# Hybrid decoder trunk, first block: where the gate constants are loaded, and the meta tokens' state as a piece of its own

## The chip, the cores and the metric

The kernel runs on one core of a Trainium2 chip. The core has five engines with a queue of instructions each: TensorE (PE in the profile, with its weight loads listed apart as PEld), VectorE (DVE), ScalarE (ACT), GpSimd (POOL) and SyncE (SP, which here does nothing but start transfers), and 16 DMA engines that all queues share. The metric is the device time of one execution in microseconds (us). A kernel's time is the median of several runs. A profile is taken of one further execution, whose own time and span are given with it.

## The reference

One layer of a hybrid decoder. Sixteen meta tokens are put ahead of 2048 tokens of 1024 channels, the rows are normalised, and one input projection feeds two branches: a Mamba-2 state-space branch (SSD, 16 heads in 4 groups, state 128) and gated linear attention (GLA, 4 heads). Each branch starts from a state that the meta tokens alone make. The branches' outputs are normalised, projected, weighted by sigmoid gates, added, projected again and added to the input.

```python
u = rmsnorm(h, norm_w)
z, xbc, dt_raw, q, k, v, g_gla, a_lr, merge_g = split_cols(u @ w_in, IN_WIDTHS)
xbc = silu(causal_depthwise_conv(xbc, conv_w, conv_b))      # -> xs, bm, cm per head
y_m, s_m = ssd_chunked(xs[:, :m], dt[:, :m], a, bm[:, :m], cm[:, :m], N_META, s0)   # meta tokens
y_r, _   = ssd_chunked(xs[:, m:], dt[:, m:], a, bm[:, m:], cm[:, m:], SSD_CHUNK, s_m)
...
gate_logit = a_lr @ gla_gate_w2 + gla_gate_b                # low-rank gates of GLA
o_m, st_m = gla_chunked(q[:, :m], k[:, :m], v[:, :m], log_a[:, :m], N_META, st0)
o_r, _    = gla_chunked(q[:, m:], k[:, m:], v[:, m:], log_a[:, m:], GLA_CHUNK, st_m)
...
return hres + (sigmoid(merge_g) * branch_proj).sum(2) @ w_out
```

## The kernel before

**Two phases.** The first goes through the 2048 tokens in four blocks of 512 (the first block has the 16 meta tokens beside them: 528 columns) and makes the branch outputs, which go to HBM. The second multiplies by the gate, branch and output weights. The change lies in the first block of the first phase.

**Products in three parts.** A weight tile is loaded raw (tile `wr`, 3 buffers, line 173), its rounded high part is made on ACT (line 163), the remainder on POOL (line 164); both lie in a tile `whl` (4 buffers). A product is three matmuls, high by high, high by low, low by high (lines 183 to 185). In the first block every weight tile is also written back to HBM in its two parts (line 179) so that later blocks can fetch it ready (line 159). The write-back lags two tiles behind: at each new tile the third last is stored, and then the new raw tile is loaded. Both are started by SP.

**Units and pieces.** A block is eight units: four SSD groups (`ssd_proj`, i from 0 to 3) and four GLA heads (`gla_proj`). A unit is a generator that yields six times. An SSD unit yields halfway through its gate projection z, after z, and after each of its four feature tiles (two of x, one each of B and C; 48 matmuls of 264 columns in the first block, evicted by ACT into `cin` and `acc`, convolved by DVE at line 477, and finished by ACT line 480 and DVE line 481 as a tile `act`). After each yield `step()` lets every running background generator go on to its own next yield. In this document the stretch from one yield to the next is a piece.

**Background work.** `ssd_scan(g)` starts when group g's projection is done and so runs beside the unit that follows. Its pieces before the change: (1) fetch the decay rows; (2) transposes and the meta tokens' inputs (lines 503 to 511), the scores of the block (522), `before(0)`; (3) `meta_state()`, then `before(1)` and `after(0)`; (4) `before(2)`, `after(1)`; (5) `before(3)`, `after(2)`; (6) `after(3)`; (7) the row norm (589) and its scaling on ACT (591); (8) transposes (596) and the store. `before(c)` is transposes (538), scalings on DVE (541 to 544) and decays on ACT and DVE (550 to 553). `after(c)` multiplies (562), reads the state `s_ssd` on PE (563), forms the chunk's own contribution (565) and updates the state. `meta_state()` is one product on PE (515) and one copy on DVE (517) that writes `s_ssd`. It runs in the first block alone. `gates` starts at unit 1 and makes the GLA gates for the whole block: transposes (419), a product with the constant `w2` (432), Abs, Exp and Ln on ACT (435, 437, 438), a subtraction and cumulative sums on DVE (441, 443).

**Order.** PE and SP run in the order in which the program is written. For ACT, DVE and POOL a planner with its own cost model fixes the order when the kernel is built. Every engine then executes its list in order: an instruction whose input is late holds up all behind it. The same is true of SP: a load whose buffer isn't free yet holds up every later load.

**Buffers that matter.** `acc` has 2 buffers; each feature tile of the convolution takes one until line 481 has read it. `act` has 8 (`NACT`); in the first block they first hold the eight transposed pieces of the input (line 291), later the feature tiles and the gates' operand. `tok4` has 5 and `cb` has 3. `late_constants()` (lines 330 to 338) loads the low-rank gate weight three times into one staging tile, makes `w2` from it on ACT and DVE, loads the masks into a `tok4` tile and casts them to bytes on DVE. It is called once, ahead of unit 1.

Of the kernel before, what the change touches and what calls it, by code (L numbers as in the profile page):

```python
# [7 lines left out]
F32 = mybir.dt.float32  # L8
# [6 lines left out]
P = 128  # L15
D = 1024
KT = 8
META = 16
BLK = 512
NCH = BLK // P  # L20
SG = 4
# [6 lines left out]
NACT = 8  # L28
# [12 lines left out]
def trunk_kernel(ctx: ExitStack, tc: tile.TileContext, xm, xmt, w_feat, w_tok, w_zm, w_br, w_o,  # L41
# [7 lines left out]
    def mk(pool, shape, dt, tag, **kw):  # L49
        cnt[0] += 1  # L50
        return pool.tile(shape, dt, tag=tag, name=f"{tag}_{cnt[0]}", **kw)
# [52 lines left out]
    for s in range(nsb):  # L104
        b = 2 * s + 2
# [12 lines left out]
    wk = first.enter_context(tc.tile_pool(name="wk", bufs=2))  # L118
# [6 lines left out]
    def bank(pool, tag):  # L125
        return mk(pool, [P, 512], F32, tag)
# [49 lines left out]
    def save(n):  # L176

        while len(unsaved) > n:
            nc.sync.dma_start(*unsaved.pop(0))
# [19 lines left out]
    def proj_tok(key, src, u, starts, banks, width=256, per=2, sub=None):  # L199

        nq = KT // per
        opened = set()
        for q0 in range(0, nq, 2):
            if q0 == nq // 2:
                yield
            ws = [load_w(f"{key}_{q}", src[:, q * per * width:(q + 1) * per * width]) for q in (q0, q0 + 1)]
            for i, ((bk, ps), a) in enumerate(zip(banks, starts)):
                c0 = sub if sub is not None and i >= NCH else 0  # L210
                for k2 in range(2 * per):
                    kt = q0 * per + k2
                    h, lo = ws[k2 // per]
                    cs = slice(k2 % per * width + c0, (k2 % per + 1) * width)
                    accum(ps[:, c0:width], tuple(t[:, kt, a:a + P] for t in u),
                          (h[:, cs], lo[:, cs]), bk not in opened, kt == KT - 1, skip_group_check=True)
                    opened.add(bk)
# [86 lines left out]
    def fetch_u(b):  # L304
        next_u[b] = yield from load_u(b)
# [22 lines left out]
    msk = const.tile([P, NMSK, P], U8, name="msk")  # L328

    def late_constants():  # L330
        w2r = mk(wk, [P, META + BLK], F32, "acc")[:48, :512]
        for i in range(3):
            nc.sync.dma_start(w2r[16 * i:16 * i + 16, :], gw2)
        nc.scalar.activation(w2, w2r, AF.Copy)
        nc.vector.tensor_tensor(w2[32:48], w2r[32:48], w2[32:48].bitcast(F32), op=ALU.subtract)
        mstg = mk(wk, [P, D], F32, "tok4", bufs=NT4)[:, :NMSK * P]
        nc.sync.dma_start(mstg, cmsk)
        nc.vector.tensor_copy(msk.rearrange("p l t -> p (l t)"), mstg)
# [109 lines left out]
    def ssd_proj(o, g):  # L448
        m0, tt = o.m0, o.tt
        feats = []  # L450
        zs = mk(wk, [P, NCH, 256], F32, "tok4", bufs=NT4)
        if g == 0:
            pss = [bank(*pl) for pl in [(pj, "pj")] * 3 + [(pt, "pt")] + ([(pc, "pc")] if m0 else [])]
            yield from proj_tok("zm", w_zm, o.u, o.starts + [0] * o.ci0, list(enumerate(pss)), 288, 1, 256)
            begin(dt_chain(o, pss[NCH:] + pss[:NCH]))
            done = [(ps[:, :256], zs[:, c]) for c, ps in enumerate(pss[:NCH])]
        else:
            pss, places = halves_of(pj, "pj")
            yield from proj_tok(f"z{g}", w_tok[g], o.u, o.starts, places)
            done = [(ps, zs[:, 2 * r:2 * r + 2].rearrange("p c f -> p (c f)")) for r, ps in enumerate(pss)]  # L460
        for ps, dst in done:
            nc.scalar.activation(dst, ps, AF.Tanh, scale=0.5)
            nc.vector.scalar_tensor_tensor(dst, dst, 1.0, ps, op0=ALU.add, op1=ALU.mult)
        yield
        for j in range(4):
            ti = g * 4 + j
            pss = proj_feat(f"s{ti}", w_feat[T_SSD + ti], o.segs_all, o.mov)
            cin = mk(wk, [P, 3 + META + BLK], F32, "cin")
            acc = mk(wk, [P, META + BLK], F32, "acc")[:, :tt]
            nc.scalar.activation(cin[:, 0:3], tails[:, ti, :], AF.Copy)  # L470
            for ps, (a, n) in zip(pss, o.segs_all):
                nc.scalar.activation(cin[:, 3 + a:3 + a + n], ps[:, :n], AF.Copy)
                nc.scalar.activation(acc[:, a:a + n], ps[:, :n], AF.Identity, scale=hcw[:, ti, 3:4],  # L473
                                     bias=hcb[:, ti:ti + 1])
            nc.gpsimd.tensor_copy(tails[:, ti, :], cin[:, tt:tt + 3])
            for k in range(3):
                nc.vector.scalar_tensor_tensor(acc, cin[:, k:k + tt], hcw[:, ti, k:k + 1], acc,  # L477
                                               op0=ALU.mult, op1=ALU.add)
            f = mk(wk, [P, META + BLK], F32, "act", bufs=NACT)
            nc.scalar.activation(f[:, :tt], acc, AF.Tanh)  # L480
            nc.vector.scalar_tensor_tensor(f[:, :tt], f[:, :tt], 1.0, acc, op0=ALU.add, op1=ALU.mult)
            feats.append(f)
            yield
        begin(ssd_scan(o, g, feats, zs))
# [7 lines left out]
    def ssd_scan(o, g, feats, zs):  # L492
# [20 lines left out]
        def meta_state():  # L513
            ps = bank(pc, "pc")
            nc.tensor.matmul(ps[:, :256], btm[:META], xw[:META].rearrange("p a c -> p (a c)"),
                             start=True, stop=True)
            nc.vector.tensor_copy(s_ssd[:, g], ps[:, :256])
# [62 lines left out]
        yield  # L580
        if m0:
            meta_state()
        for c in range(1, NCH):
            before(c)
            after(c - 1)
            yield
# [15 lines left out]
    def gla_proj(o, h):  # L602
        m0 = o.m0
        t0 = T_GLA + 4 * h
        qs = mk(wk, [P, META + BLK], F32, "act", bufs=NACT)
        ps, = proj_feat(f"g{t0}", w_feat[t0], o.segs_real, o.mov)
        nc.scalar.activation(qs[:, :BLK], ps, AF.Copy, scale=QSCALE)
        yield
        kf = mk(wk, [P, META + BLK], F32, "act", bufs=NACT)
        for ps, (a, n) in zip(proj_feat(f"g{t0 + 1}", w_feat[t0 + 1], o.segs_all, o.mov), o.segs_all):  # L610
            nc.scalar.activation(kf[:, a:a + n], ps[:, :n], AF.Copy)
        yield
        vh = mk(wk, [P, NCH, 256], F32R, "tok4", bufs=NT4)
        vl = mk(wk, [P, NCH, 256], F32R, "tok4", bufs=NT4)
        vm = None
        pss, places = halves_of(pj, "pj")
        if m0:
            vm = mk(wk, [P, 256], F32, "c1", bufs=NC1)[:META]
            pv5 = bank(pt, "pt")
            places.append((2, pv5[:, :256]))  # L620
        yield from proj_tok(f"v{h}", w_tok[SG + h], o.u, o.starts + [0] * o.ci0, places)
        if m0:
            nc.scalar.activation(vm, pv5[:META, :256], AF.Copy)
        for r, ps in enumerate(pss):
            split(*[t[:, 2 * r:2 * r + 2].rearrange("p c f -> p (c f)") for t in (vh, vl)], ps)
        yield
        gs = []
        for j in range(2):
            ps, = proj_feat(f"g{t0 + 2 + j}", w_feat[t0 + 2 + j], o.segs_real, o.mov)
            gg = mk(wk, [P, BLK], F32, "gg", bufs=4)  # L630
            nc.scalar.activation(gg, ps, AF.Tanh, scale=0.5)
            nc.vector.scalar_tensor_tensor(gg, gg, 1.0, ps, op0=ALU.add, op1=ALU.mult)
            gs.append(gg)
            yield
        begin(gla_scan(o, h, qs, kf, (vh, vl), vm, gs))
# [174 lines left out]
    def begin(gen):  # L810
        begun.append(gen)

    def step():
        running.extend(begun)
        begun.clear()
        for gen in list(running):
            if next(gen, running) is running:
                running.remove(gen)
# [7 lines left out]
    with tc.manual_schedule(engines={mybir.EngineType.PE, mybir.EngineType.SP}):  # L826
        for b in range(nblk):
            o = new_block(b, next_u[b])
            for i in range(SG + GH):
                if (b, i) in beside:  # L830
                    begin(beside_unit(beside[b, i]))
                if (b, i) == (0, 1):
                    late_constants()
                if i == 1:
                    begin(gates(o))
                if i == SG and b + 1 < nblk:
                    begin(fetch_u(b + 1))
                for _ in ssd_proj(o, i) if i < SG else gla_proj(o, i - SG):
                    step()
            save(0)  # L840
        while running or begun:
            step()
# [221 lines left out]
    for key, st in zip(late, (stages[0], stages[-4])):  # L1064
        i, end = begins[stages.index(st)] + 9, begins[stages.index(st) + 1] - 16
# [106 lines left out]
```

## Time and profile before

| | |
|---|---|
| median of 3 runs | 2349.48 us (2349.11 to 2352.76) |
| profiled execution | 2353.29 us, its span 2351.5 us |
| mean granted TensorE clock | 0.982 of full |
| busy: PE, DVE, ACT, POOL | 2251.0, 1547.5, 1181.6, 672.9 us |
| moved by DMA | 518.05 MB, 220 GB/s on the mean |

The profile has a page of totals and views of the trace. In the timelines a row is start, duration, engine, line, operation, output<-inputs, shape and count, and in brackets the idle time just ahead of it with what ended that. "SPq" and "ACTq" are transfers as their queue starts them. In the table of windows a row is a stretch, its length, then busy time (and count) of PE, PEld, DVE, ACT and POOL, the clock granted to TensorE as a share of full speed, the mean busy share of the DMA engines, and GB/s.

### The profile page before, as it was taken

The numbers are of one execution on the slowest core, as the hardware profiler recorded it, in microseconds if no ns is written. First come the engines' busy times: TensorE is split into PE (matmuls) and PEld (weight loads), VectorE is DVE, ScalarE is ACT, GpSimd is POOL, SyncE is SP. The second block draws the span as 40 slices with busy tenths as digits, with TensorE's granted clock in tenths as the row PEclk, the third lists the DMA queues.
The fourth block names the chain that finished last, engine by engine and source line by source line (L and its number), as shares of the span: only waits on it lengthen the run. The fifth ranks groups of instructions, "written<-read, shape, count | busy, mean of one in ns | idle before, by whom it ended". The sixth has DMA issues, their size and how long they took to land.

```text
span 2351.5 us, 36473 instructions
## 1 busy us (share of the span) xinstructions
PE 2251.0 (96%) x12641; PEld 1962.2 (83%) x12641; DVE 1547.5 (66%) x2895; ACT 1181.6 (50%) x2758; POOL 672.9 (29%) x681
## 2 busy tenths in 40 slices
PE   7799999999999999999999999879999999999998
PEld 7689889889888988888988898768878788888786
DVE  5576665676675567566568655674578854778866
ACT  5565655465534455543456443464455454554543
POOL 4343433122321212221122200207423354423331
PEclk9899999999999999999999999989999999999999
DMA  7665875666786676777677654447577876777753
GB/s 270 225 206 184 299 252 193 204 218 223 240 274 191 205 223 219 238 258 224 194 225 221 205 174 157 154 135 254 194 242 261 297 236 203 251 272 252 254 165 122
DMA packets 301545, 518.05 MB, mean 220 GB/s; under 512 B 27696, under 2 KB 143664, under 8 KB 301360
## 3 DMA queue, kind: packets, MB, share of 16 engines
q1 hardware_dynamic: 200400, 402.84, 52.9%
q10 hardware_dynamic: 100960, 112.88, 13.8%
q8 instruction: 99, 1.62, 0.3%
q14 instruction: 86, 0.70, 0.1%
HBM read 368.42 MB, written 147.19 MB: 219 GB/s over the span
## 4 chain that ended last, share of the span: by engine, by line
PE 48%; DMA 6%; DVE 6%; ACT 3%; issue 2%; SPq 1%; POOL 1%; ACTq 0%; DVEq 0%; POOLq 0%
PE pj L183 6%; PE pj L185 6%; PE pj L184 6%; PE psa L183 4%; PE psa L185 4%; PE psa L184 4%; PE psb L184 2%; PE psb L185 2%; PE psb L183 2%; DVE b L893 1%; DMA br<-br_t 1%; PE psc L183 1%; PE psc L185 1%; PE psc L184 1%; PE pc L562 1%
## 5 line engine op out<-in xcount | busy, mean ns | idle before, releaser
L183 PE MATMUL pj<-u,whl 128*128 128x512 f32 (+1 forms) x1184 | 447.9, 378 | 10.5 <-ACT whl L163 3.5
L185 PE MATMUL pj<-u,whl 128*128 128x512 f32 (+1 forms) x1184 | 431.8, 365 | 0.8 <-POOL whl L164 0.8
L184 PE MATMUL pj<-u,whl 128*128 128x512 f32 (+1 forms) x1184 | 430.8, 364 | 0.0
L183 PE MATMUL pj<-whl,u 128*128 128x256 f32 (+1 forms) x992 | 290.3, 293 | 8.2 <-ACT whl L163 6.7
L185 PE MATMUL pj<-whl,u 128*128 128x256 f32 (+1 forms) x992 | 283.4, 286 | 1.5 <-DVE u L298 1.4
L184 PE MATMUL pj<-whl,u 128*128 128x256 f32 (+1 forms) x992 | 283.4, 286 | 1.0 <-POOL whl L164 1.0
L183 PEld LDWEIGHTS pj<-u,whl 128*128 128x128 f32 x1184 | 225.9, 191 | 48.8 <-ACT whl L163 3.9
L183 PE MATMUL psa<-b,a 128*128 128x512 f32 x640 | 249.8, 394 | 11.1 <-ACT sn L930 8.2
L185 PEld LDWEIGHTS pj<-u,whl 128*128 128x128 f32 x1184 | 224.9, 190 | 36.9 <-POOL whl L164 1.1
L184 PEld LDWEIGHTS pj<-u,whl 128*128 128x128 f32 x1184 | 225.5, 190 | 33.6
L185 PE MATMUL psa<-b,a 128*128 128x512 f32 x640 | 251.3, 393 | 1.2 <-DVE a L914 1.2
L184 PE MATMUL psa<-b,a 128*128 128x512 f32 x640 | 251.0, 392 | 0.0
L183 PEld LDWEIGHTS pj<-whl,u 128*128 128x128 f32 x992 | 191.2, 193 | 9.4 <-ACT whl L163 6.9
L184 PEld LDWEIGHTS pj<-whl,u 128*128 128x128 f32 x992 | 191.0, 193 | 2.1 <-POOL whl L164 1.6
L185 PEld LDWEIGHTS pj<-whl,u 128*128 128x128 f32 x992 | 190.8, 192 | 2.2 <-DVE u L298 2.2
L893 DVE TENSOR_TENSOR b<-br,b 128x512 fp32r<-128x512 f32 x196 | 153.1, 804 | 56.2 <-ACT b L892 55.7
L80 POOL TENSOR_TENSOR wr<-wr 128x256 f32<-128x256 f32 x80 | 65.1, 814 | 425.5 <-DMA wr<-y 169.7
L904 POOL TENSOR_TENSOR as<-ar,ar 128x512 f32<-128x512 f32 x40 | 57.8, 1446 | 447.5 <-DMA ar<-in_w_br 191.2
L164 POOL TENSOR_TENSOR whl<-wr,whl 128x512 fp32r<-128x512 f32 (+1 forms) x100 | 132.9, 1335 | 182.5 <-ACT whl L163 155.2
L892 ACT ACTIVATE b<-br 128x512 fp32r<-128x512 f32 x196 | 119.2, 626 | 112.3 <-DMA br<-br_t 41.5
L914 DVE TENSOR_TENSOR a<-ar,a 128x512 fp32r<-128x512 f32 x160 | 131.8, 839 | 64.4 <-ACT a L913 64.1
L477 DVE SCALAR_TENSOR_TENSOR acc<-cin,hcw,acc 128x512 f32<-128x512 f32 (+1 forms) x192 | 154.6, 805 | 27.0 <-ACT acc L473 26.3
(271 smaller groups left out, 5062.7 us busy)
## 6 DMA issues: line engine op xcount, KB each, us to landing
whl<-k_s SPq DMA_DIRECT2D x96, 512.0 KB, 4.5
whl<-k_g SPq DMA_DIRECT2D x96, 512.0 KB, 4.2
whl<-k_v SPq DMA_DIRECT2D x48, 512.0 KB, 3.7
whl<-k_z SPq DMA_DIRECT2D x36, 512.0 KB, 3.8
wr<-in_w_feat SPq DMA_DIRECT2D x64, 256.0 KB, 4.2
k_s<-whl SPq DMA_DIRECT2D x32, 512.0 KB, 3.7
cb<-cumd ACTq DMA_DIRECT2D x64, 256.0 KB, 5.4
y<-gg ACTq DMA_DIRECT2D x64, 256.0 KB, 4.5
```

What stands on the lines that cost most here:

```text
L80: nc.gpsimd.tensor_tensor(o, x, y, op=ALU.subtract)
L164: nc.gpsimd.tensor_tensor(hl[:, 1], raw, hl[:, 0].bitcast(F32), op=ALU.subtract)
L183: nc.tensor.matmul(ps, sh, mh, start=first, stop=False, **kw)
L184: nc.tensor.matmul(ps, sh, ml, start=False, stop=False, **kw)
L185: nc.tensor.matmul(ps, sl, mh, start=False, stop=last, **kw)
L477: nc.vector.scalar_tensor_tensor(acc, cin[:, k:k + tt], hcw[:, ti, k:k + 1], acc, op0=ALU.mult, op1=ALU.add)
L562: nc.tensor.matmul(py[:, h * 64:(h + 1) * 64], dm[:, h], xdt[:, h], start=True, stop=True)
L892: nc.scalar.activation(t[:, 0], raw, AF.Copy)
L893: nc.vector.tensor_tensor(t[:, 1], raw, t[:, 0].bitcast(F32), op=ALU.subtract)
L904: nc.gpsimd.tensor_tensor(s1, a21, a22, op=ALU.add)
L914: nc.vector.tensor_tensor(t[:, 1], src, t[:, 0].bitcast(F32), op=ALU.subtract)
```

## The change

Two edits, both of which act in block 0 alone. The gate weight's staging tile is taken from the `act` buffers in place of an `acc` buffer, and `late_constants()` is called one unit earlier: after the second yield of unit 0, that is after the z projection of group 0 and ahead of its first feature tile. And `ssd_scan` yields once more right behind `meta_state()`, so that in block 0 a scan has nine pieces: the meta state is piece 3 alone, and `before(1)` with `after(0)` and everything behind them come one piece later than they did. What is computed stays the same.

```diff
     def late_constants():
-        w2r = mk(wk, [P, META + BLK], F32, "acc")[:48, :512]
+        w2r = mk(wk, [P, META + BLK], F32, "act", bufs=NACT)[:48, :512]
         for i in range(3):
             nc.sync.dma_start(w2r[16 * i:16 * i + 16, :], gw2)
...
         if m0:
             meta_state()
+            yield
         for c in range(1, NCH):
             before(c)
             after(c - 1)
...
-                if (b, i) == (0, 1):
-                    late_constants()
                 if i == 1:
                     begin(gates(o))
...
-                for _ in ssd_proj(o, i) if i < SG else gla_proj(o, i - SG):
+                for n, _ in enumerate(ssd_proj(o, i) if i < SG else gla_proj(o, i - SG)):
                     step()
+                    if (b, i, n) == (0, 0, 1):
+                        late_constants()
             save(0)
```

## The prediction

> **What bounds the kernel now.** I read the page first, for the engine that is nearly always busy:
>
> ```profile
> span 2351.5 us, 36473 instructions
> ...
> PE 2251.0 (96%) x12641; PEld 1962.2 (83%) x12641; DVE 1547.5 (66%) x2895; ACT 1181.6 (50%) x2758; POOL 672.9 (29%) x681
> ```
>
> TensorE is the bound, so a change this small in work is worth only the time in which PE idles or runs at a low clock. The windows show such time early in block 0:
>
> ```profile
> 20.00:40.00 20.00, 20.00 (x159) 19.92 (x158) 7.56 (x23) 10.37 (x26) 10.45 (x9) 1.00 0.96 327
> 60.00:65.00 5.00, 0.00 (x0) 0.00 (x0) 3.61 (x6) 2.40 (x6) 0.18 (x1) 0.98 0.85 268
> 65.00:70.00 5.00, 2.53 (x8) 1.95 (x9) 0.62 (x1) 1.38 (x3) 2.53 (x2) 0.50 1.04 408
> 100.00:105.00 5.00, 2.54 (x8) 2.19 (x9) 4.76 (x16) 2.26 (x7) 0.78 (x1) 0.50 0.68 211
> 145.00:150.00 5.00, 5.00 (x23) 4.55 (x24) 2.14 (x5) 4.17 (x11) 2.50 (x2) 0.50 0.59 197
> ```
>
> From 60 to 65 PE does nothing, and after this gap, after the one that ends in the window from 100 and after the one ahead of 145, the granted clock is 0.50. The PE timeline names the gaps:
>
> ```profile
> 39.64 0.34 PE L390 MATMUL pt<-dx,cst 128*128 128x80 f32 x2
> ...
> 66.42 0.58 PE L183 MATMUL pj<-whl,u 128*128 128x256 f32 x1 [6.66 <-ACT whl L163]
> ...
> 75.83 0.49 PE L419 MATMUL pt<-cst,alr 128*48 128x128 f32 x3
> 76.08 0.37 PE L183 MATMUL pj<-whl,u 128*128 128x256 f32 x1
> ...
> 81.87 0.49 PE L506 MATMUL pt<-cst,act 128*16 128x128 f32 x3
> ...
> 84.19 0.39 PE L183 MATMUL pj<-u,whl 128*128 128x264 f32 x1
> 87.93 0.39 PE L183 MATMUL pj<-u,whl 128*128 128x264 f32 x1 [3.10 <-ACT g_all L435]
> ...
> 95.11 0.69 PE L515 MATMUL pc<-c,bt 16*128 16x256 f32 x2
> ...
> 102.46 1.22 PE L563 MATMUL pc<-s_ssd,act 128*128 128x256 f32 x2 [5.33 <-DVE s_ssd L517]
> ...
> 110.78 0.49 PE L538 MATMUL pt<-cst,act 128*128 128x128 f32 x3
> ...
> 144.04 2.53 PE L596 MATMUL pt<-cst,tok 128*128 128x128 f32 x8 [2.89 <-ACT tok L591]
> ```
>
> The gap of 6.66 is the start of unit 1 (weights of z, group 1); the gap of 5.33 is `after(0)` waiting for the meta tokens' state. The SP queue says why the weights are late; its rows of the timeline, then its waits:
>
> ```profile
> 26.61 0.56 SPq L173 DMA_DIRECT2D wr<-in_w_feat  x1
> ...
> 41.94 0.42 SPq L173 DMA_DIRECT2D wr<-in_w_feat  x1
> 58.64 1.25 SPq L333 DMA_DIRECT2D acc<-in_gw  x3
> 59.93 0.42 SPq L337 DMA_DIRECT2D tok<-in_cmsk  x1
> ...
> 60.93 0.38 SPq L173 DMA_DIRECT2D wr<-in_w_tok  x1
> ```
>
> ```profile
> SPq L333 <- DVE act L481: 15.6, 1, 15.6
> ```
>
> and what it waited for, on DVE:
>
> ```profile
> 57.90 0.71 DVE L481 SCALAR_TENSOR_TENSOR act<-act,acc 128x528 f32<-128x528 f32 x1 [0.77 <-ACT act L480]
> ```
>
> The gate weight's staging tile needs an `acc` buffer, and that comes free only when DVE has finished group 0's third feature tile (line 481). For 15.6 us SP waits with every later load behind it, and the first weights of unit 1 leave at 60.93, when PE has already run dry at 66.42 - 6.66 = 59.76. Who delays the meta state is seen on DVE, and the work ahead of it on ACT:
>
> ```profile
> 95.95 2.40 DVE L441 TENSOR_TENSOR tok<-tok,g_all 128x528 f32<-128x528 f32 x2 [1.70 <-ACT g_all L438]
> 98.27 3.81 DVE L443 TENSOR_TENSOR_SCAN g_all<-ones_r,tok 128x16 f32<-128x16 f32 x10
> 102.01 0.39 DVE L517 COPY s_ssd<-pc 128x256 f32<-128x256 f32 x1
> ```
>
> The copy (517) is ready soon after its product at 95.11, but DVE has been told to do the gates' subtractions and sums first. PE comes to line 563 within the same piece, and nothing covers it.
>
> **Edit 1, the constants earlier and through `act`.** It takes away the 15.6 us wait. The staging tile now takes an `act` buffer. All eight held the transposed input; these rows are the last that used it, on DVE and on ACT's queue:
>
> ```profile
> 22.10 1.94 DVE L298 TENSOR_TENSOR u<-act,u 128x528 fp32r<-128x528 f32 x3
> ...
> 21.87 0.33 ACTq L297 DMA_DIRECT2D u<-act  x1
> ```
>
> At 26, where SP now stands (its load at 26.61 is the one behind), seven or eight of them are free. The masks' `tok4` buffers were read for the input's row norms, before all this. Neither waits.
>
> Then SP goes straight from the load at 41.94 to unit 1's, held only by the `wr` and `whl` buffers. Both come free in time (transfers of the first 100 us: count, size, median time to landing; then POOL's timeline):
>
> ```profile
> wr<-in_w_tok SPq DMA_DIRECT2D x4, 256.0 KB, 4.9
> ...
> tok<-in_cmsk SPq DMA_DIRECT2D x1, 448.0 KB, 3.9
> ...
> acc<-in_gw SPq DMA_DIRECT2D x3, 32.0 KB, 1.8
> ```
>
> ```profile
> 49.03 1.35 POOL L164 TENSOR_TENSOR whl<-wr,whl 128x512 fp32r<-128x512 f32 x1 [0.70 <-ACT whl L163]
> ```
>
> POOL has dealt with the last feature tile of unit 0 at 50.4, so the three raw buffers are free by then, and with the 4.9 us from issue to landing that such loads took in the first 100 us the z weights are there by 55; `whl` buffers follow PE, half a tile (2.95 us) behind one another. PE gets z's first two quarters before 59.76. So z should take its full-speed time. In its second half that is 76.08 to 81.87, 5.79; the first half took 66.42 to 75.83, 9.41, for the same 48 matmuls, 3.62 too many (low clock, and weights that still came one by one). Gain: 6.66 + 3.62 = **10.3 us**.
>
> The clock part can be set against a rule. The Trainium skill ("TensorE: Matmul & The Clock Gate", Part 1: The HAM clock gate) says that an idle window of some 3.4 us halves the clock and a busy one of the same length restores it. That is an estimated loss of 1.7 us for each long gap. Behind the gap of 5.33 the trace agrees (1.7, below); behind that of 6.66 it shows up to 3.6. By the page's figure the sum below would come to 13.7 in place of 15.6.
>
> What edit 1 adds is ahead of unit 0's features: four transfers on SP (1.25 + 0.42 = 1.67 us of issue) that carry 3 x 32 + 448 KB = 0.557 MB, in a stretch where the DMA engines are 0.96 busy at 327 GB/s: 1.70 us. Behind them are queued the raw tile issued at 26.61 and all later ones. How tight that is:
>
> ```profile
> 31.63 1.29 POOL L164 TENSOR_TENSOR whl<-wr,whl 128x512 fp32r<-128x512 f32 x1 [2.10 <-ACT whl L163]
> ...
> 33.74 0.37 PE L183 MATMUL pj<-u,whl 128*128 128x264 f32 x1
> ```
>
> The tile's low part was done at 32.92, PE took it at 33.74: 0.8 spare. Bounds: at best its load loses only the 1.67 of issue, of which 0.8 is spare, 0.9; at worst issue and bytes add up, 3.37 - 0.8 = 2.6. I take the middle, **1.7 us lost**; later tiles had more to spare (SP had been waiting for buffers, not data). The cast on ACT and two operations on DVE stay as many:
>
> ```profile
> 61.35 0.63 ACT L334 ACTIVATE w<-acc 48x512 fp32r<-48x512 f32 x1 [0.32 <-DMA acc<-in_gw]
> ```
>
> They go to a stretch in which ACT waits for weights to cast (10.4 of 20 us busy) and DVE has 7.6 of 20; that cover gone, they cost 0.6 on the first tile's path.
>
> **Edit 2, the meta state apart.** It adds no instruction. PE does line 515, then a whole feature tile (48 matmuls, by unit 0's first 33.74 to 39.64 = 5.90 us), then 538, 562 and 563. Counted from the start of piece 2 (81.87 before): line 515 (0.69) at 13.24, 538 at 13.24 + 0.69 + 5.90 = 19.8, and line 563 after 538 and 562, which before took from 95.80 to 102.46 - 5.33 = 97.13, so at 21.2. If ACT and DVE keep their order, the copy is done at 102.40 - 81.87 = 20.5. So the wait goes, with 0.6 to spare. Before, the feature tile behind 563 ended at 110.78, that is 28.9; now the same work is done at 21.2 and an estimated 0.7 for 563 and 565 (the row of 563 has 1.22 at clock 0.50; half of it, and a little) = 21.9. Gain: 28.9 - 21.9 = **7.0 us** (5.33 of wait, 1.7 of clock). Should the gap of 3.10 (a PSUM bank held until ACT's 435) close too, PE would only come sooner to 563 and wait there for the same DVE chain; so I count that gap at nothing.
>
> Groups 1 to 3 had no wait at 563; for them the edit only moves `before(1)` and all behind it by a piece. Cost bounds: it may take away the wait at 144.04 (2.89, and 5 us at clock 0.50, 2.5: 5.4), since line 596 no longer shares its piece with the next group's piece 2; or it may bring a wait of that kind to other groups. I take 0 and keep both ends. I counted buffers piece by piece: `act` reaches exactly 8 in unit 1 (four old feature tiles, three new, the gates' operand, which is free when the fourth needs its place), `tok4` exactly 5 in unit 5. No wait, but nothing to spare.
>
> **Sum.** 10.3 + 7.0 - 1.7 = 15.6 us. Against the profiled execution's own 2353.29 (span 2351.5, 1.8 around it) that is 2337.7; the median of the runs lies 3.8 below that execution, so 2349.48 - 15.6 = **2333.9**. PE has 96% over the whole, so what is saved early should reach the end.
>
> **Rivals.**
>
> *Only the loads.* The planner makes a new order for ACT and DVE. If it sets something more ahead of the copy (517), the wait at 563 comes back one piece later; the spare is 0.6. Then 2349.5 - 10.3 + 1.7 = 2340.9. For it: the copy stood behind ten sums before. Against: it is now written a piece earlier than what needs it.
>
> *More goes.* The wait at 144.04 goes as well: 2333.9 - 5.4 = 2328.5; with the first tile losing only 0.9, 2327.7. For it: its piece loses half of its crowd. Against: line 591 waited for the row norm's own chain, which moves along.
>
> *Nothing to gain.* ACT takes over as the bound of units 1 and 2, and what PE saves it waits for later. The planner's cast of a weight (163) then stands behind the decays. Some 13 of the 15.6 come back: about 2347. Against: ACT has only 50% over the whole.
>
> *Slower.* Each scan's row norm and scaling (piece 8 now) falls into the same piece as the next group's transposes and decays, and the transposes behind it (596) follow one feature tile later. ACT's rows for that:
>
> ```profile
> 83.23 1.56 ACT L550 ACTIVATE sq<-cb,tkc 128x128 f32<-128x128 f32 x5
> ...
> 89.39 0.61 ACT L552 ACTIVATE sq<-sq 128x512 f32<-128x512 f32 x1
> ...
> 143.48 1.71 ACT L591 ACTIVATE tok<-tok,rstd 128x256 f32<-128x256 f32 x4 [2.68 <-POOL rstd L227]
> ```
>
> If ACT runs all 16 decays (0.31 each, 5.0) and four Exps (2.4) and some four casts and evictions (0.6 each by line 334's row, 2.4) first, line 591 ends 5.0 + 2.4 + 2.4 + 1.7 = 11.5 after the piece starts, while PE is at 596 after 84.19 - 81.87 = 2.3 and a tile of 5.9, 8.2: 3.3 idle, and a slow clock after it as costly as after the first gap, 3.6. At four places 27.6, less the 5.4 of today's: 22.2 lost against 15.6 gained, 2349.5 + 6.6 = 2356.1. It decides where the four places together cost over 21, 5.2 each. For it: one such wait exists. Against: the scan is written ahead of the next group's work in each step, and the wait of today came from the row norm, not from decays.
>
> *Not what it says.* The staging tile could still wait, for an input tile's store in place of line 481. That is over by about 27, so it costs under 1 and lies in the bounds of edit 1.
>
> **How the numbers follow.** Forecast 0.52 (its own range 2327 to 2340: the bounds of the first tile, some 2 of clock, and up to 5 for the new order); only the loads 0.14; more goes 0.12; nothing to gain 0.10; slower 0.12. The range with 8 in 10 goes from 2325 to 2348 and leaves out the slower case and tails. A run can tell 0.2% (4.7 us) from no change. Faster than 2344.8: the first three, 0.78, less their upper tails, 0.77. Within: most of "nothing to gain" and the slower case's near end, 0.10. Slower: 0.13.
>
> **What would show it.** SP's loads of the gate weight at about 26, and no SP wait of 15 us. The first z weights of unit 1 issued before 50; PE without a gap near 60 and with clock 1.00 there; line 506 of unit 1 near 73. The first feature tile of unit 0 up to 2.6 later than 33.74. Line 563 a piece behind 515 and without a wait over 1 us. Wrong would be: a wait of the same size at another line of units 1 to 3 (ACT's 163 or 591 named as releaser), or block 0 shorter by 15 and the end not.

## The result, and the profile after

| | before | after |
|---|---|---|
| median (6 runs each) | 2349.59 us (2345.52 to 2352.76) | 2336.12 us (2334.76 to 2339.70) |
| profiled execution | 2353.29, span 2351.5 | 2339.70, span 2337.9 |

The ratio is 0.9944, with a 95% interval from 0.9932 to 0.9957: the change makes the kernel 13.5 us faster by the medians. The forecast was 15.6 us, 2333.9.

The total is close to the sum, but not for the reasons of every term. Four places of the trace show it. First SP's queue, where the constants are loaded now (timeline of the changed kernel; start, duration, transfer):

```profile
25.98 1.36 SPq L333 DMA_DIRECT2D act<-in_gw  x3
27.39 0.42 SPq L337 DMA_DIRECT2D tok<-in_cmsk  x1
...
28.47 1.44 SPq L173 DMA_DIRECT2D wr<-in_w_feat  x1
...
49.75 0.42 SPq L173 DMA_DIRECT2D wr<-in_w_tok  x1
```

The gate weight leaves at 25.98, nothing makes SP wait for it, and unit 1's first weights leave at 49.75 in place of 60.93. TensorE of the changed kernel, the rows that answer to those of the prediction:

```profile
36.55 0.59 PE L183 MATMUL pj<-u,whl 128*128 128x264 f32 x1 [1.61 <-ACT whl L163]
...
37.90 0.59 PE L185 MATMUL pj<-u,whl 128*128 128x264 f32 x1 [0.53 <-DVE dw L380]
...
45.97 0.34 PE L390 MATMUL pt<-dx,cst 128*128 128x80 f32 x2
...
77.33 0.49 PE L506 MATMUL pt<-cst,act 128*16 128x128 f32 x3
...
83.39 0.39 PE L183 MATMUL pj<-u,whl 128*128 128x264 f32 x1 [3.11 <-ACT g_all L435]
...
90.56 0.69 PE L515 MATMUL pc<-c,bt 16*128 16x256 f32 x2
...
98.55 0.65 PE L563 MATMUL pc<-s_ssd,act 128*128 128x256 f32 x2
...
147.28 0.59 PE L183 MATMUL pj<-u,whl 128*128 128x264 f32 x1 [4.19 <-ACT acc L473]
...
401.85 1.04 PE L802 MATMUL pt<-cst,ot 128*128 128x128 f32 x8
...
1541.55 1.22 PE L183 MATMUL psa<-b,a 128*128 128x512 f32 x2 [1.88 <-ACT b L893]
```

The last two rows are the transposes of the second GLA head of block 0 and the first product of the second phase. Before they stood here:

```profile
413.80 1.04 PE L801 MATMUL pt<-cst,ot 128*128 128x128 f32 x8
...
1558.83 1.22 PE L183 MATMUL psa<-b,a 128*128 128x512 f32 x2 [1.91 <-ACT b L892]
```

Set side by side with the rows of before, this is the account (minus is earlier than before):

| up to | before | after | shift so far | this stretch |
|---|---|---|---|---|
| end of unit 0's first feature tile (390) | 39.64 | 45.97 | +6.3 | +6.3 |
| unit 1, piece 2 (506) | 81.87 | 77.33 | -4.5 | -10.9 |
| `before(1)`, `after(0)` and the tile beside the wait | 110.78 | 99.3 | -11.5 | -7.0 |
| second GLA head of block 0 (801, now 802) | 413.80 | 401.85 | -12.0 | -0.5 |
| start of the second phase | 1558.83 | 1541.55 | -17.3 | -5.3 |
| end of the span | 2351.5 | 2337.9 | -13.6 | +3.7 |

(99.3 is 98.55 and some 0.7 for lines 563 and 565.) The two gains are there, 10.9 for 10.3 and 7.0 for 7.0. The loss ahead of unit 0's features is 6.3 and not 1.7. The windows show what it consists of, and that the clock near 60 is full now:

```profile
34.00:36.00 2.00, 0.95 (x9) 0.85 (x8) 1.54 (x6) 1.07 (x7) 0.00 (x0) 1.00 0.73 264
36.00:38.00 2.00, 0.91 (x3) 0.61 (x3) 1.27 (x2) 1.97 (x4) 1.26 (x1) 0.61 0.04 14
38.00:40.00 2.00, 2.00 (x9) 2.00 (x10) 1.65 (x4) 1.28 (x3) 1.16 (x1) 0.50 0.73 256
40.00:42.00 2.00, 2.00 (x11) 2.00 (x10) 0.22 (x1) 0.00 (x0) 1.36 (x2) 0.50 0.89 285
...
60.00:65.00 5.00, 5.00 (x43) 5.00 (x43) 3.71 (x4) 2.31 (x5) 3.02 (x3) 1.00 0.79 269
```

PE waits 1.61 for the first tile's high part and 0.53 for its low part (the second row names DVE, but POOL's line 164 ended just then, at 37.84), and works at clock 0.50 until 43. Of the 6.3, 1.2 is there when z ends (34.94, before 33.74), 1.6 is the first wait, and 3.5 is the tile itself, which takes 9.42 in place of 5.90: 0.5 in the second wait, the rest at the slow clock. Note the DMA column from 36 to 38: 0.04. The transfers are through; what is late then is no longer data. ACT says what it did:

```profile
28.97 0.64 ACT L334 ACTIVATE w<-act 48x512 fp32r<-48x512 f32 x1 [0.24 <-DMA act<-in_gw]
32.03 0.38 ACT L462 ACTIVATE tok<-pj 128x256 f32<-128x256 f32 x1 [2.42 <-PE pj L185]
...
35.71 0.27 ACT L377 ACTIVATE de<-dx 128x80 f32<-128x80 f32 x1
35.87 0.63 ACT L163 ACTIVATE whl<-wr 128x512 fp32r<-128x512 f32 x1
```

Before, the cast of the first feature tile (163, at 30.92) stood in ACT's list ahead of the evictions of z (462). Now the planner has put it behind all of them, and each of these has to wait for PE to finish a part of z. How much is data and how much is order can be read off, since the trace has the time from issue to landing of every load. Before, the tile's first half was issued at 26.61, landed 4.2 later at 30.8 and was cast at once. Here it was issued at 28.47, landed 4.7 later at 33.2, and was cast at 35.87: the data came 2.4 later, and the order added 2.7. The second half landed at 35.6 (before 32.9) and was cast at 38.15.

The 1.2 is older than the constants: PE reached the short products of 32 columns at the end of z's first weight tile at 21.64 before and at 22.62 here. Its products were 0.24 us apart at first and 0.13 later, and here the first of these lasted longer. The clock column reads 1.00 in both, so the trace doesn't name the cause. In the executions below z ends between 33.6 and 34.9; differences of 1 us in line 390 alone mean nothing.

### The profile page after: what moved, and what is told of

It is laid out like the page before. It is cut to its first block, busy times and chain, and to the rows that moved or that the text cites. A ratio compares the mean times of both kernels' runs of the same rounds, so it can differ in the third digit from the quotient of the medians.

```text
span 2337.9 us, 36478 instructions
## 1 busy us (share of the span) xinstructions
PE 2247.7 (96%) x12641; PEld 1959.0 (84%) x12641; DVE 1548.3 (66%) x2895; ACT 1180.1 (50%) x2758; POOL 673.3 (29%) x681
```

## The experiments

Three questions: are the two edits' gains separate terms; why did the early load cost three times its price; and what is the extra piece worth in each group. Traces are compared at fixed points of PE's work, one execution for each kernel, since the medians of one kernel scatter by several us. The ratio is to runs of before taken in the same round. In kernels with a line added the numbers of later lines are up to 5 higher. All points are starts in PE's timeline of the profiled execution:

| kernel | line 390 | unit 1, 506 | second GLA head | second phase | median | ratio to before (95%) |
|---|---|---|---|---|---|---|
| before | 39.64 | 81.87 | 413.80 | 1558.83 | 2349.6 | |
| after | 45.97 | 77.33 | 401.85 | 1541.55 | 2336.1 | 0.9932 to 0.9957 |
| edit 1 alone | 44.39 | 77.03 | 409.20 | 1553.04 | 2348.0 | 0.9979 to 1.0014 |
| edit 2 alone | 39.50 | 81.86 | 405.62 | 1540.23 | 2340.1 | 0.9937 to 0.9969 |
| buffer changed, old place | 40.05 | 81.79 | 403.07 | 1539.84 | 2339.4 | 0.9942 to 0.9974 |
| masks late | 40.49 | 74.85 | 396.65 | 1538.75 | 2336.7 | 0.9913 to 0.9965 |
| gate weight late | 44.71 | 85.65 | 410.80 | 1551.05 | 2346.2 | 0.9981 to 1.0001 |
| first tile's load first | 44.82 | 76.83 | 402.83 | 1537.20 | 2325.4 | 0.9889 to 0.9924 |
| cast on POOL | 43.67 | 78.30 | 405.97 | 1539.55 | 2335.9 | 0.9936 to 0.9971 |
| masks late, piece in group 0 only | 40.91 | 74.12 | 401.97 | 1534.05 | 2338.9 | 0.9937 to 0.9986 |
| masks late, no piece in group 1 | 40.82 | 74.64 | 393.27 | 1534.22 | 2330.4 | 0.9904 to 0.9941 |
| constants a piece later | 39.75 | 81.49 | 403.87 | 1538.65 | 2338.2 | 0.9921 to 0.9965 |

### Edit 1 alone

```diff
             meta_state()
-            yield
```

> Edit 1 without edit 2: constants early through act, the scan's pieces as before. Theory 'separate terms': the gap at the start of unit 1 goes (10.3 to 10.9 gained, as between the two profiles), the first feature tile ends some 6 us later (line 390 at about 46 in place of 39.64), and the wait of about 5 us at line 563 for the meta state stays. Sum 2349.6 - 10.6 + 6 = about 2345. Rival 'the early loss belongs to the new piece': the first feature tile ends near 40 and the time is about 2339. Rival 'the gap was not SP's': the gap near 60 stays and the time is 2349 or more.

Separate terms, as expected; the time is 3 us above what I added up from them (2348.0 for 2345). The gap near 60 is gone, line 390 is late (44.39), and the wait for the meta state stays:

```profile
97.07 1.22 PE L563 MATMUL pc<-s_ssd,act 128*128 128x256 f32 x2 [3.64 <-DVE s_ssd L517]
```

Block 0 is 4.6 ahead at the second GLA head. Alone, edit 1 loses 4.8 up to line 390 and gains 9.6 from there to unit 1's line 506, and the timed runs can't tell it from before.

### Edit 2 alone

```diff
-        w2r = mk(wk, [P, META + BLK], F32, "act", bufs=NACT)[:48, :512]
+        w2r = mk(wk, [P, META + BLK], F32, "acc")[:48, :512]
...
+                if (b, i) == (0, 1):
+                    late_constants()
...
-                    if (b, i, n) == (0, 0, 1):
-                        late_constants()
```

> Edit 2 without edit 1: the gate weight still takes an acc buffer ahead of unit 1. Theory 'separate terms': SP's wait of 15 us and the gap near 60 stay, the wait at 563 in group 0 goes (7.0 gained), and in group 1 a wait for the eviction of a feature tile (line 473, about 4 us and a slow clock) takes the place of the one at 596: about 2342 to 2344. Rival 'the new wait in group 1 comes from the earlier start': no wait over 1 us for line 473 in group 1, and 2338. Rival 'the piece is worth nothing alone': 2347 to 2350.

PE's timeline has the old gap and the new wait side by side:

```profile
66.49 0.58 PE L183 MATMUL pj<-whl,u 128*128 128x256 f32 x1 [6.87 <-ACT whl L163]
...
150.44 0.59 PE L183 MATMUL pj<-u,whl 128*128 128x264 f32 x1 [4.22 <-ACT acc L473]
```

The wait at 563 has gone, and the 4.2 us in group 1 come from the piece and not from the earlier start. Block 0 gains 8.2. The two edits' gains there, 4.6 + 8.2 = 12.8, add up to about the 12.0 of both. By the timed runs edit 2 alone gives most of what both give: its ratio, 0.9937 to 0.9969, overlaps that of the changed kernel, and 2340.1 is 2 below the time expected.

### The buffer changed, the call left at its old place

```diff
+                if (b, i) == (0, 1):
+                    late_constants()
...
-                    if (b, i, n) == (0, 0, 1):
-                        late_constants()
```

> As the changed kernel, but the constants are called at their old place ahead of unit 1, through an act buffer. Theory 'early load costs': SP doesn't wait, the first feature tile is back near its old place (line 390 at 39.6 to 41), line 506 of unit 1 near 71 to 72, and the time is 2336.1 - 5.3 = about 2331. Rival 'they must be early': ahead of unit 1's weights the same four transfers delay z by some us, a gap near 60 of 1 to 5 us, and the time is 2334 to 2340.

Half of my theory held: line 390 is back at 40.05. The other half was wrong, and the time is the rival's. SP's wait of 15.6 us is gone (3.0 is left at line 333), and yet unit 1 starts with a gap:

```profile
65.75 0.58 PE L183 MATMUL pj<-whl,u 128*128 128x256 f32 x1 [5.59 <-ACT whl L163]
```

Taking SP's wait away doesn't suffice. It isn't the transfers that the rival named either: the first of z's raw tiles, issued at 56.02, landed at 59.3, and ACT cast it at 65.08, behind line 480 (63.92) and the gate weight's cast (64.56). The same order is shown in rows two kernels further on.

### Masks late, gate weight early

```diff
+    def late_masks():
         mstg = mk(wk, [P, D], F32, "tok4", bufs=NT4)[:, :NMSK * P]
...
+                if (b, i) == (0, 1):
+                    late_masks()
```

> As the changed kernel, but the masks (448 KB, one transfer, one cast on DVE) are loaded at the old place ahead of unit 1; the gate weight (96 KB, three transfers) stays early. Theory 'bytes': without the masks the first feature tile's weights come 1.4 us sooner, most of the early loss goes, line 390 near 41, about 2332. Theory 'ACT order': the planner puts the cast of the first feature tile behind the evictions of z because of the gate weight's transfers and cast ahead of it; then line 390 stays near 45 and the time near 2336.

Line 390 is at 40.49, and block 0 is 17.2 ahead of before, 5.2 ahead of the changed kernel. In ACT's timeline the first tile's cast is back ahead of the evictions of z (464 here), with the gate weight's cast ahead of both:

```profile
31.03 0.63 ACT L334 ACTIVATE w<-act 48x512 fp32r<-48x512 f32 x1 [2.36 <-DMA act<-in_gw]
32.30 0.63 ACT L163 ACTIVATE whl<-wr 128x512 fp32r<-128x512 f32 x1 [0.64 <-DMA wr<-in_w_feat]
32.84 0.95 ACT L464 ACTIVATE tok<-pj 128x256 f32<-128x256 f32 x3
```

From the end of z (34.59) to line 390 it takes 5.90, as before. So it is the masks' load of 448 KB that brings the early loss, and not the gate weight (the masks' cast on DVE moved with the load; the two weren't separated). The median, 2336.7, is no lower than the changed kernel's 2336.1, where I expected 2332. Of the 5.2 us, 2.8 are left at the start of the second phase (1538.75 against 1541.55); why the later blocks give back the rest isn't shown.

### Gate weight late, masks early

```diff
+    def late_masks():
         mstg = mk(wk, [P, D], F32, "tok4", bufs=NT4)[:, :NMSK * P]
...
+                if (b, i) == (0, 1):
+                    late_constants()
...
-                        late_constants()
+                        late_masks()
```

> As the changed kernel, but the gate weight is loaded and cast at the old place ahead of unit 1 (through act); the masks stay early: one transfer of 448 KB, nothing added to ACT there. Theory 'bytes, by way of the planner's order': the masks alone delay the first feature tile's weights, the planner again sets their cast behind the evictions of z, and line 390 stays at 44 to 46. Theory 'the gate weight's three transfers and cast': line 390 near 41. At unit 1 the three small transfers ahead of z's weights should leave no gap over 2 us. Time about 2336 by the first, 2332 by the second.

The counterpart agrees on the masks: line 390 at 44.71. That unit 1 would have no gap was wrong, and so the time is 2346.2 and not 2336. Here is the reason for the gap of 5.59. Rows of SP, ACT and PE:

```profile
63.03 0.33 SPq L173 DMA_DIRECT2D wr<-in_w_tok  x1
```

```profile
68.31 0.64 ACT L482 ACTIVATE act<-acc 128x528 f32<-128x528 f32 x1 [2.50 <-DVE acc L479]
68.86 0.19 ACT L472 ACTIVATE cin<-tails 128x3 f32<-128x3 f32 x1
68.95 0.61 ACT L334 ACTIVATE w<-act 48x512 fp32r<-48x512 f32 x1
69.47 1.65 ACT L163 ACTIVATE whl<-wr 128x512 fp32r<-128x512 f32 x3
```

```profile
70.14 0.58 PE L183 MATMUL pj<-whl,u 128*128 128x256 f32 x1 [5.59 <-ACT whl L163]
```

Three raw tiles are cast without a break at 69.47; the first of them had landed at 59.5 and the last, issued at 63.03, at 67.5. ACT had idled 2.50 for DVE to finish unit 0's last feature tile. The planner has put the gate weight's cast behind that tile's line 480 (482 here), and z's casts behind the gate weight.

### The first tile's load ahead of the constants

```diff
                     if (b, i, n) == (0, 0, 1):
+                        raws[f"s0_0"] = load_raw(w_feat[T_SSD][:, :512])
                         late_constants()
```

> As the changed kernel, but the raw load of the first feature tile's first half is started ahead of the constants, by name, so that only the later halves are behind them. Theory 'one late tile': the first half is cast ahead of the evictions of z as before the change, PE has no gap near 35; the second half is now the late one, with a gap up to 2 us near 37 and line 390 at 41 to 44. Rival 'the whole stretch is short of bytes': line 390 stays at 45 to 46 in any order. Time 2331 to 2334 by the first, 2336 by the rival.

The first half is cast at 31.03, as before the change, and PE has no gap near 35. But the second half, now the one behind the masks, landed at 36.0 and is cast at 38.41, behind z's evictions, and PE waits 1.45 and 0.92 there; line 390 at 44.82 lies between the two expectations. Moving the order only hands the lateness on. The median of 2325.4 is the lowest of all and lower than either theory's; its ratio, 0.9889 to 0.9924, lies clear of the changed kernel's. Block 0 doesn't explain it: at the second GLA head this kernel is 1.0 behind the changed one, and 4.4 ahead of it when the second phase starts. What the later blocks gained there wasn't tried, so the cause of the largest gain on record stays open.

### The first tile cast by POOL

```diff
-            nc.scalar.activation(hl[:, 0], raw, AF.Copy)
+            if key == "s0_0":
+                nc.gpsimd.tensor_copy(hl[:, 0], raw)
+            else:
+                nc.scalar.activation(hl[:, 0], raw, AF.Copy)
```

> As the changed kernel, with the same transfers in the same order, but the high part of the first feature tile's first half is cast by POOL, which has nothing to do there, and so doesn't stand in ACT's list behind the evictions of z. Theory 'ACT's order': PE's gap near 35 to 36.6 shrinks to under 0.8, the slow clock after it (0.50 from 38 to 42) goes or is short, line 390 at 41.5 to 43.5 in place of 45.97. Theory 'data too late': the raw tile isn't there before 35, and line 390 stays at 45 to 46.

With the same transfers in the same order, POOL casts the tile as soon as it is there; then ACT's next casts and PE:

```profile
33.63 0.61 POOL L164 CAST whl<-wr 128x512 fp32r<-128x512 f32 x1 [3.89 <-DMA k_zm<-whl]
```

```profile
38.78 1.13 ACT L166 ACTIVATE whl<-wr 128x512 fp32r<-128x512 f32 x2
```

```profile
39.45 0.39 PE L186 MATMUL pj<-u,whl 128*128 128x264 f32 x1 [0.85 <-ACT whl L166]
...
40.89 0.39 PE L188 MATMUL pj<-u,whl 128*128 128x264 f32 x1 [0.93 <-POOL whl L167]
```

The raw tile landed at 33.5 and POOL took it at 33.63, while ACT took it at 35.87 in the changed kernel. The gap near 36 is down to 0.22 and the slow clock behind it is gone; line 390 stands at 43.67, a little above my 43.5, with z ending at 34.94 in both executions. So ACT's order in the first half is worth 2.3 of the loss. The rest is the second half: it landed at 35.6, 2.7 later than before, and ACT cast it at 38.78, 3.2 after it had landed. The 2.3 don't last: a wait of 1.47 with a slow clock behind it follows at 46.59, at line 506 this kernel is 1.0 behind the changed one, at the second GLA head 4.1, and the median is the same.

### Constants one piece later

```diff
-                    if (b, i, n) == (0, 0, 1):
+                    if (b, i, n) == (0, 0, 2):
```

> As the changed kernel, but all constants are called one piece later, behind the first feature tile of unit 0 in place of ahead of it. In ACT's list the gate weight's cast, and behind it the casts of the second feature tile's weights, now come after the first feature tile's line 480. Theory 'ACT's order, not the bytes': the first feature tile is back at its old place (line 390 at 39.5 to 41), and PE then waits 5 us or more for line 163 ahead of the second feature tile, until line 480 has run near 46 to 48, with the raw weights long there. Theory 'bytes': the wait there is under 2.5 us. Time 2336 to 2340 by the first, 2331 to 2333 by the second.

The sharpest test of order against bytes. SP's last load in this stretch, ACT and PE:

```profile
34.93 1.05 SPq L173 DMA_DIRECT2D wr<-in_w_feat  x1
```

```profile
44.73 0.64 ACT L480 ACTIVATE act<-acc 128x528 f32<-128x528 f32 x1 [0.48 <-DVE acc L477]
45.28 0.61 ACT L334 ACTIVATE w<-act 48x512 fp32r<-48x512 f32 x1
45.80 1.66 ACT L163 ACTIVATE whl<-wr 128x512 fp32r<-128x512 f32 x3
```

```profile
46.46 0.59 PE L183 MATMUL pj<-u,whl 128*128 128x264 f32 x1 [5.69 <-ACT whl L163]
```

The last of the three raw tiles was asked for at 34.93 and landed at 41.2, the first at 37.4; ACT cast all three at 45.80, right behind line 480 and the gate weight, and PE stood still for 5.69 from 40.77. Here it is the order and not the data. What the early constants had gained at unit 1 is lost again (81.49 at line 506).

### The piece in group 0 only, and in all groups but 1

On the kernel with the masks late.

```diff
             meta_state()
-            yield
+            if g == 0:
+                yield
```

> As the kernel with the masks late and the gate weight early, but the extra piece is made in group 0 alone. Theory 'the new wait in group 1 (line 473, 4.2 us) is the price of the piece there': it goes, group 1's wait for the decays' or the row norm's chain at 596 (2.9 us) may come back, and the end of block 0 lies within 4 us of that kernel's, to either side. Rival 'the piece is worth something in every group': block 0 ends 5 us or more later, as groups 1 to 3 lose it. Time 2328 to 2340.

The 4.2 us at line 473 went, but the rival was right: block 0 ends 5.3 later than with the piece in all groups (401.97 against 396.65), and two waits of before came back:

```profile
225.43 0.59 PE L183 MATMUL pj<-u,whl 128*128 128x264 f32 x1 [2.46 <-ACT whl L163]
...
287.15 0.66 PE L718 MATMUL pt<-cst,act 128*128 128x128 f32 x4 [2.10 <-ACT gg L602]
```

The second kernel has `if g != 1` in the same place.

> As the kernel with the masks late and the gate weight early, but the extra piece is made in groups 0, 2 and 3, not in group 1. Theory 'the wait of 4.2 us at line 473 in group 1 is the price of the piece in that group, and the piece is worth something in groups 2 and 3': that wait goes, the waits near 225 (ACT's 163) and near 287 (transposes behind ACT's 598) stay away, block 0 ends 3 to 6 us before that kernel's, and the time is 2328 to 2333. Rival 'the waits move with the new order': another wait of 3 us or more in groups 1 or 2 takes its place, block 0 ends within 2 us of that kernel's or later, 2335 to 2338.

As the theory had it: no wait at 473, both waits above stay away, and block 0 ends 3.4 before the kernel with all pieces, 8.6 before the changed kernel. One smaller wait came in group 1:

```profile
143.40 0.70 PE L565 MATMUL pc<-s_ssd,act 128*128 128x256 f32 x2 [1.74 <-DVE s_ssd L519]
```

Its median of 2330.4 is 5.7 below the changed kernel's, though the intervals of the ratios (0.9904 to 0.9941 and 0.9932 to 0.9957) still touch.

## Why the prediction was right, and where it wasn't

**The gap at unit 1: right in size, with 10.9 for 10.3, and half right in mechanism.** SP's wait for an `acc` buffer was there, but it wasn't the only thing that held z's weights: the gap goes only because the gate weight's cast has moved too. With the buffer alone changed the gap was 5.59 instead of 6.66, as ACT's list held z's casts behind line 480. The first half of z now takes 5.76 (65.28 to 71.04), full speed as forecast. That is 3.4 gained and not 3.62: the row at 75.83 is what the window left of a group of five transposes that starts at 75.58. Another 0.8 is unit 0's later tiles, which take 19.3 up to z in place of 20.1. Line 506 came at 77.33, where I had named 73, because of the next term.

**The first feature tile: the term was mis-sized.** The step "at best 0.9, at worst 2.6, I take 1.7" counted SP's issue and the bytes. It measured 6.3 in the changed kernel and 4.8 with edit 1 alone, and 5.1 and 4.3 counted from the end of z, outside both bounds. For the data alone the bounds were sound: the first half landed 2.4 later, with 0.8 to spare. They left out that the planner orders ACT anew around a later load: the cast went behind the evictions of z (35.87, where POOL could have it at 33.63), and the short waits brought the clock to 0.50 for several us, which I had priced only for long gaps. The sentence that the casts "cost 0.6 on the first tile's path" saw the instructions that were added, not those that were moved by them.

**The meta state: right, 7.0.** Counted from the start of piece 2, line 563 runs at 98.55 - 77.33 = 21.2, the number forecast. The copy is done on DVE at 97.05, 19.7 after the start, where I had 20.5:

```profile
90.56 2.41 DVE L441 TENSOR_TENSOR tok<-tok,g_all 128x528 f32<-128x528 f32 x2 [1.71 <-ACT g_all L438]
92.89 3.84 DVE L443 TENSOR_TENSOR_SCAN g_all<-ones_r,tok 128x16 f32<-128x16 f32 x10
96.65 0.40 DVE L517 COPY s_ssd<-pc 128x256 f32<-128x256 f32 x1
```

DVE kept the order that caused the wait; the feature tile now covers it. The wait of 3.10 for line 435 stayed (3.11), as assumed. Edit 2 alone takes the wait away as well, so the cause is shown.

**Groups 1 to 3: zero in sum, but of large parts.** Near zero (-0.5) is what came out, out of a new wait of 4.19 with a slow clock behind it, and of three waits that went: 2.89 at 144.04, and these two of before:

```profile
238.01 0.39 PE L183 MATMUL pj<-u,whl 128*128 128x264 f32 x1 [3.49 <-ACT whl L163]
...
298.74 0.66 PE L714 MATMUL pt<-cst,act 128*128 128x128 f32 x4 [2.10 <-ACT gg L598]
```

I had not considered the last two. Smaller new waits came too, the largest 1.25 at 111.21 with the clock at 0.50 behind it. The rival "slower" had the right engine and the wrong line: ACT's decays (550) did hold something up, in group 1 alone, and it was the eviction of a feature tile. The four decays ahead of it waited 0.72 for the transfer of their rows (`cb`):

```profile
145.22 1.28 ACT L550 ACTIVATE sq<-cb,tkc 128x128 f32<-128x128 f32 x4 [0.72 <-DMA cb<-cumd]
146.40 0.37 ACT L472 ACTIVATE cin<-pj 128x264 f32<-128x264 f32 x1
146.67 0.56 ACT L473 ACTIVATE acc<-pj,hcb,hcw 128x264 f32<-128x264 f32 x1
```

**What the sum didn't contain.** Blocks 1 to 3 aren't touched by either edit, yet they were 5.3 us shorter in the profiled execution; ACT's and DVE's lists differ there too. The kernel with edit 2 alone gained 10.4 there (8.2 to 18.6 ahead), the one with edit 1 alone 1.2. The second phase was 3.7 longer (796.4 for 792.7); over all twelve profiled executions it lies between 786 and 798, so that is no effect I can assign. The forecast's nearness to the total owes much to luck, to these two and the early loss cancelling: 6.3 - 1.7 = 4.6 too much lost, 5.3 gained in later blocks. Nor was the split right. The sum had 10.3 - 1.7 = 8.6 for edit 1 and 7.0 for edit 2. With edit 2 in both kernels, edit 1 is worth 3.8 at the second GLA head (405.62 to 401.85) and nothing at the start of the second phase (1540.23 to 1541.55).

## What to carry to other kernels

Where a planner orders some engines, moving a transfer moves more than the transfer: look at each engine's list on both sides of the new place, and price the instructions that now stand behind others, since an engine that takes its list in order waits at the first late entry while ready work stands behind it. Move the few bytes that something needs and leave the large ones where nobody waits: the gate weight early and the masks late was ahead at the end of block 0 (396.65, against 401.85 with both early and 403.07 with both late), though its median isn't below that of both early. An extra piece between producer and consumer is worth measuring group by group, because the same shift covered a wait in one group and made one in the next.

## What the runs showed of the hardware

In the changed kernel the granted clock was 0.71 from 36 to 37 and 0.50 from 37 to 43. The first product behind the wait of 1.61 (36.55) already took 0.59; one of the same shape takes 0.39 at full clock (83.39). By the Trainium skill ("TensorE: Matmul & The Clock Gate", Part 1: The HAM clock gate) an idle window of some 3.4 us is what halves it. Here a wait of half that length went with a halved clock. From 34 to 38 PE was busy 1.86 of 4 us. The length of a single wait doesn't decide it in these traces. Waits of 0.85 and 0.93 within 2.4 us in the kernel with the cast on POOL left the clock at 1.00, from 38 to 42 with PE busy 2.21 of 4 us. Behind the wait of 3.11 in the changed kernel the first product still ran at full clock; the clock was 0.61 from 84 to 85 and 0.50 from 85 to 87. So a short wait can cost as much as a long one; from what amount of idling on isn't settled by these runs.

One kernel's runs scatter more than I had taken: before ranged over 2341.9 to 2358.6 in the 26 runs of one round. Differences of 5 us between kernels show in the traces at fixed points of block 0 and not in single medians.
